# First modulation round of the first layer's mixing: weighted sums on VectorE instead of matmuls on TensorE, at the beginning of the mixing

## The chip, the cores and the metric

The kernel runs on one core of a Trainium2 chip. A core has TensorE (PE in the rows; PEld is its weight load), VectorE (DVE), ScalarE (ACT), GpSimd (POOL) and SyncE (SP), each with an instruction queue of its own that it works through in order; engines wait for one another through semaphores. The metric is the device time of one execution in microseconds.

## What is computed

A diffusion backbone of two layers over 512 latent tokens and 256 context tokens of width 1024, in fp32. Each layer gets six modulation vectors per stream from a small product:

```python
def modulation(cvec, w_mod, b_mod):
    m = (jax.nn.silu(cvec) @ w_mod + b_mod)[..., None, :]
    return jnp.split(m, 6, axis=-1)
...
    sh1, sc1, ga1, sh2, sc2, ga2 = modulation(c, w_mod, b_mod)
    sh1c, sc1c, ga1c, sh2c, sc2c, ga2c = modulation(c_ctx[None], w_mod, b_mod)
    u = (rmsnorm(x, g_mix) * (1 + sc1) + sh1) @ w_in
    ...
    x = x + ga1 * mix
    x = x + ga2 * squared_relu_mlp(rmsnorm(x, g_mlp) * (1 + sc2) + sh2, w_up, w_down)
```

`c` is the conditioning vector of the latent tokens, `c_ctx` that of the context. `w_mod` is 1024x6144 per layer, 24 MB, read for just two vectors. In the middle of a layer stands the mixing: pooling, a bidirectional gated linear attention (GLA) and softmax attention, side by side, on slices of `u`.

## The kernel before, in words

**Tiling.** Activations lie with channels on the partitions (`hT`, eight tiles), each split in a high part, rounded to fp32r, and a low rest; weights are split likewise (`whi` by ScalarE at L159, `wlo` by VectorE at L78), and a product is three matmul passes: high by high, low by high, high by low. `fm_matmul` (L321, L323) gives channel-major results (`fm`, a latent and a context matmul per pass), `tm_matmul` (L340) token-major ones (`tm`).

**Modulation.** It goes in three rounds of two vectors each (2048 columns of `w_mod`). Round 0 (shift and scale of the mixing) of the first layer is computed at the very start. Rounds 1 (mixing gate, MLP shift) and 2 (MLP scale, MLP gate) of the first layer are the thread `mods`, which `mod_rest` makes of two `modulation_round`s (L181): per 128 rows of `w_mod` two tiles `rawm` of 128x1024 are loaded and used at once as the moving operand of four matmuls with the stationary `sstat` (L190), which holds the two conditioning vectors in two of 32 columns; four column groups of the array sum into one PSUM tile `pm`. `mod_end` (L194) adds the bias (`brow`), transposes and writes `modT` and, for a gate, rows in DRAM (`gaD`). The second layer's rounds already go the other way: `modulation_sums` (L211) multiplies and adds the tiles on VectorE into `macc`, one accumulator per stream (the first product by ScalarE, L227, the others L229), and leaves to TensorE just a matmul with a column of ones (`osel`, L238) that sums over the partitions.

**Mixing.** Four threads are written as generators: `"a"` projects (q and k of GLA head pair 1, two gates, then keys and values, queries, pooling), `"g"` is the GLA of both head pairs, `"m"` the modulation, `"t"` the softmax attention. The string `STEPS[0]` names the thread that takes the next step. The steps of `"g"` begin with `decay` (L663) of pair 0, one step per direction: a matmul pair `z` (L670, L671), ScalarE and VectorE in turn (`z`, `e`: L674 to L679), and a tree of products on GpSimd; `levels` (L728) then multiplies the queries by both decays into `QQ` (L771, L772) and computes eight levels of products `att` (L769); the zero level reads `gq` and `KK`, the first one both halves of `QQ`. The gates (`gate_proj`, L642) have a chain of their own on the same engines (`sg`, `gate`).

**What sets the order.** The string gives the order of writing. From it a scheduler with a timeline of its own makes the order of each engine's queue, so work of several threads is interleaved more finely than the string says. Buffers bind it: `wp` holds five tiles each of the tags `hi` and `lo`, shared by weights and `rawm` tiles, and three of `raw`, shared by weights as they come in and `brow`; the accumulators and activations come from 29 tiles of `sp`; of the PSUM pools, `psB` has three tiles and `psA` two. All loads named here stand in SyncE's queue.

Of the kernel before, what the change touches and what calls it, by code (L numbers as in the profile page):

```python
# [10 lines left out]
F32 = mybir.dt.float32  # L11
F32R = mybir.dt.float32r
I32 = mybir.dt.int32
AF = mybir.ActivationFunctionType
ALU = mybir.AluOpType
# [6 lines left out]
KT = 8  # L22
# [2 lines left out]
LEVELS = (1, 2, 4, 8, 16, 32, 64)  # L25
C_GV, C_GG, C_R, C_AQ = 768, 1024, 1280, 1312
GT = 5
STEPS = ("agamagamgaamgaagmaagmagamagamagamagagamagamagamagamgaamgaagmaagmagamagamttgtgttg"
         "tgttgtttgttgttttgttttgtt",
         "aaggggagaggaaagaaggaaaaaagaaaagaaaggaagaaggatatgatttttgaatgt"  # L30
         "tgtttgggtttgttggttttgtttgt")

# [2 lines left out]
def hybrid_kernel(ctx, tc, x, c, cx, c_ctx, w_mod, b_mod, g_mix, w_in, w_pool, s_pool, w_gate, b_gate,  # L35
                  g_gla, g_q, g_k, w_out, g_mlp, w_up, w_down, g_final, k_mask, k_rope, k_edge, k_invw, out):
    nc = tc.nc
    V, A, G, T = nc.vector, nc.scalar, nc.gpsimd, nc.tensor
# [3 lines left out]
    wp = ctx.enter_context(tc.tile_pool(name="wp", bufs=5))  # L42
# [9 lines left out]
    def nm(s):  # L52
        uid[0] += 1
        return f"{s}_{uid[0]}"

    def slot(s, dt=F32, w=NT):
        return sp.tile([128, w], dt, tag="S", name=nm(s))
# [16 lines left out]
    def psC(s):  # L74
        return pc.tile([128, 512], F32, tag="pc", name=nm(s))
# [11 lines left out]
    ident = const.tile([128, 128], F32, name="ident")  # L87
    make_identity(nc, ident)

    osel = const.tile([128, 2, 32], F32, name="osel")  # L90
# [21 lines left out]
    sstat = const.tile([128, KT, 32], F32, name="sstat")  # L112
# [65 lines left out]
    gaD = dp.tile([2, 2, 2, D], F32, name="gaD")  # L178
    xD = dp.tile([NL, D], F32, name="xD")

    def modulation_round(l, r, modT):  # L181
        pm = psC("pm")
        for k in range(KT):
            yield
            for h in range(2):
                raw = wp.tile([128, 1024], F32, tag="lo" if h else "hi", name=nm("rawm"))
                c0 = r * 2048 + h * 1024
                nc.sync.dma_start(raw, w_mod[l, k * 128:(k + 1) * 128, c0:c0 + 1024])
                for j in (2 * h, 2 * h + 1):
                    T.matmul(pm[32 * j:32 * j + 32, :], sstat[:, k, :], raw[:, (j % 2) * 512:(j % 2) * 512 + 512],  # L190
                             start=(k == 0), stop=(k == KT - 1), skip_group_check=True)
        mod_end(l, r, modT, pm)

    def mod_end(l, r, modT, pm):  # L194
        brow = wp.tile([128, 1024], F32, tag="raw", name=nm("brow"), bufs=3)[:, 0:512]
        for j in range(4):
            c0 = r * 2048 + j * 512
            nc.sync.dma_start(brow[32 * j:32 * j + 32], b_mod[l, c0:c0 + 512].partition_broadcast(32))
        V.tensor_tensor(brow, pm, brow, ALU.add)
        pt = psC("pt")  # L200
        for cc in range(4):
            T.transpose(pt[:, cc * 128:(cc + 1) * 128], brow[:, cc * 128:(cc + 1) * 128], ident)
        V.tensor_copy(modT[:, r], pt.rearrange("p (c j r) -> p j c r", c=4, j=4)[:, :, :, 0:2])
        if r >= 1:
            which = r - 1
            for s in range(2):
                for jj in range(2):
                    row = 32 * (jj + (2 if r == 2 else 0)) + s
                    nc.gpsimd.dma_start(gaD[l, which, s:s + 1, jj * 512:(jj + 1) * 512], brow[row:row + 1, :])

    def modulation_sums(l, r, modT, streams):  # L211
# [27 lines left out]
                             start=(s == 0), stop=(s == streams - 1), skip_group_check=True)  # L239
        mod_end(l, r, modT, pm)  # L240

    def mod_vec(modT, idx, s):

        r, j0 = idx // 2, (idx % 2) * 2
        return modT[:, r, j0:j0 + 2, :, s]
# [142 lines left out]
    def fin_scale(l, M, which):  # L388
        modT, scT, shT = M
        o = l * NV + 8 * which  # L390
        g_ = vec[:, o:o + 8].rearrange("p (j c) -> p j c", j=2)
        for s in range(2):
            V.scalar_tensor_tensor(scT[:, which, s].rearrange("p (j c) -> p j c", j=2), mod_vec(modT, 3 * which + 1, s),
                                   1.0, g_, ALU.add, ALU.mult)
            V.tensor_copy(shT[:, which, s].rearrange("p (j c) -> p j c", j=2), mod_vec(modT, 3 * which, s))
# [12 lines left out]
                next(other, None)  # L408

    def mod_rest(l, M):  # L410
        yield from modulation_round(l, 1, M[0])
        yield from modulation_round(l, 2, M[0])
        fin_scale(l, M, 1)

# [9 lines left out]
    for l in range(2):  # L424
# [7 lines left out]
        modT, scT, shT = MODS[l]  # L432
        hT = hT1 if l else new_hT("hT")
        if l == 0:
# [4 lines left out]
            rawm = {}  # L439
# [136 lines left out]


        mods = mod_rest(0, MODS[0]) if both else iter(())
        tstack = ExitStack()
        LT = layer_tables(l, tstack.enter_context(tc.tile_pool(name=f"ta{l}", bufs=1)))  # L580
# [554 lines left out]
        ths = {"g": gla_thread(), "a": at_, "m": mods, "t": att_}  # L1135
        for ch in STEPS[l]:
            if ch == "t":
# [13 lines left out]
        for p2 in range(len(live) // 2):  # L1151
            XP[p2] = bp.tile([128, 2, D], F32, tag=f"X{p2}", name=nm("X"))
            t0 = 2 * p2 * 128
            src = xD[t0:t0 + 256] if l else (x[0, t0:t0 + 256] if p2 < 2 else cx[0])
# [187 lines left out]
```

## Time and profile before

| | us |
|---|---|
| median of 3 runs | 1671.8 |
| lowest, highest | 1671.43, 1680.17 |
| the profiled execution | 1671.28 |
| its span in the profile | 1669.1 |
| mean granted TensorE clock (1 is full) | 0.985 |

The profile is of one execution; times in its rows count from the start of its span. A row of the timeline has the start, the duration, the engine, the line of the kernel, the operation, result and operand by tile names, shapes and count, and in brackets the idle time before it with what ended it. A record is one instruction of the trace; an fp32 matmul leaves two. In the span the first layer's beginning lies from 0 to about 60 us, its mixing from there to about 340, of which the softmax attention starts at about 220.

### The profile page before, as it was taken

To read this page: it belongs to the slowest core of one execution; us is meant where nothing else is said; L and a number is where in the kernel's file an instruction comes from. 1 tells how busy PE (TensorE), PEld (TensorE's weight loads), DVE (VectorE), ACT (ScalarE), POOL (GpSimd) and SP (SyncE) were. 2 spreads that over 40 slices of the span, in tenths; PEclk is the share of its full clock that TensorE was granted. 3 is DMA by queue.
4 is the path that set the end of the run, shared out by engine and by line. 5 is a ranking of instruction groups with operands and counts; after the bars stand their busy time and mean duration, and the time that the engine had idled before them with its cause. 6 is when DMAs were issued, how large, how long until landed. Compare 5 with 4: busy or idle time off the path is not lost.

```text
span 1669.1 us, 27434 instructions
## 1 busy us (share of the span) xinstructions
PE 1595.7 (96%) x11403; PEld 1306.2 (78%) x11403; DVE 923.3 (55%) x1330; ACT 630.9 (38%) x1074; POOL 406.4 (24%) x476
## 2 busy tenths in 40 slices
PE   7999979999999999999999999897999999999997
PEld 4888856678888888888888789785667888888886
DVE  5437666753673654636546563587763545455554
ACT  5545445561531312213113234555662523223332
POOL 1121311212303041130321462241201122222224
PEclk9999989999999999999999999998999999999999
DMA  9445400222340422515424332100032313333331
GB/s 330 128 135 175 149 2 7 98 93 59 102 139 26 141 97 59 176 50 172 150 65 170 103 108 81 40 2 2 33 121 75 111 54 101 101 101 101 101 101 51
DMA packets 136636, 163.31 MB, mean 98 GB/s; under 512 B 9908, under 2 KB 108608, under 8 KB 136512
## 3 DMA queue, kind: packets, MB, share of 16 engines
q1 hardware_dynamic: 130176, 148.41, 27.9%
q10 hardware_dynamic: 5824, 13.12, 2.1%
q8 instruction: 89, 1.46, 0.4%
q14 instruction: 35, 0.29, 0.1%
q0 software_dynamic: 512, 0.03, 0.0%
HBM read 157.31 MB, written 4.23 MB: 97 GB/s over the span
## 4 chain that ended last, share of the span: by engine, by line
PE 84%; DVE 6%; ACT 4%; DMA 2%; issue 2%; POOL 2%; SPq 0%; ACTq 0%; DVEq 0%; POOLq 0%
PE dn L340 25%; PE up L321 19%; PE tm L340 7%; PE op L340 6%; PE up L323 5%; PE fm L321 4%; PE av L1071 3%; PE pT L1054 2%; PE up L330 2%; PE fm L323 1%; PE sc L1033 1%; PE att L769 1%; PE sc L1034 1%; DVE nmx L1036 1%; PE pm L190 1%
## 5 line engine op out<-in xcount | busy, mean ns | idle before, releaser
L159 ACT ACTIVATE whi<-raw 128x1024 fp32r<-128x1024 f32 (+2 forms) x182 | 185.3, 1033 | 568.0 <-PE dn L340 293.0
L1194 POOL TENSOR_TENSOR X<-X,rtmp 128x512 f32<-128x512 f32 x158 | 216.1, 1370 | 640.4 <-DVE rtmp L1193 640.1
L78 DVE TENSOR_TENSOR wlo<-raw,whi 128x1024 fp32r<-128x1024 f32 (+2 forms) x182 | 223.6, 1237 | 213.4 <-ACT whi L159 211.7
L1193 DVE TENSOR_TENSOR rtmp<-dn,ga 128x512 f32<-128x512 f32 x160 | 109.5, 689 | 212.8 <-PE dn L340 211.3
L340 PE MATMUL dn<-whi,ah 128*128 128x512 f32 x480 | 187.3, 390 | 0.6 <-ACT whi L159 0.6
L340 PE MATMUL dn<-whi,al 128*128 128x512 f32 x480 | 187.2, 390 | 0.0
L340 PE MATMUL dn<-wlo,ah 128*128 128x512 f32 x480 | 186.2, 390 | 0.0
L321 PE MATMUL up<-h2h,whi 128*128 128x512 f32 x464 | 182.5, 393 | 1.5 <-ACT relu L1240 1.5
L321 PE MATMUL up<-h2h,wlo 128*128 128x512 f32 x464 | 182.9, 394 | 0.0
L321 PE MATMUL up<-h2l,whi 128*128 128x512 f32 x464 | 182.4, 393 | 0.0
L340 PEld LDWEIGHTS dn<-whi,ah 128*128 128x128 f32 x480 | 90.1, 188 | 22.0 <-ACT whi L159 1.0
L321 PEld LDWEIGHTS up<-h2h,whi 128*128 128x128 f32 x464 | 87.1, 188 | 24.1 <-ACT relu L1240 1.7
L340 PEld LDWEIGHTS dn<-wlo,ah 128*128 128x128 f32 x480 | 90.1, 188 | 19.5 <-DVE wlo L78 0.5
L340 PEld LDWEIGHTS dn<-whi,al 128*128 128x128 f32 x480 | 90.1, 188 | 19.4
L340 PE MATMUL tm<-whi,hTh 128*128 128x256 f32 (+1 forms) x352 | 102.3, 292 | 1.1 <-ACT UV L891 1.1
L321 PEld LDWEIGHTS up<-h2h,wlo 128*128 128x128 f32 x464 | 87.1, 188 | 19.6
L321 PEld LDWEIGHTS up<-h2l,whi 128*128 128x128 f32 x464 | 87.1, 188 | 19.3
L340 PE MATMUL tm<-whi,hTl 128*128 128x256 f32 (+1 forms) x352 | 100.7, 287 | 0.0
L340 PE MATMUL dn<-whi,a 128*128 128x512 f32 x320 | 100.0, 395 | 0.4 <-DVE rtmp L1193 0.4
L340 PE MATMUL tm<-wlo,hTh 128*128 128x256 f32 (+1 forms) x352 | 100.2, 288 | 0.0
L229 DVE SCALAR_TENSOR_TENSOR macc<-rawm,sstat,macc 128x1024 f32<-128x1024 f32 x56 | 76.3, 1383 | 8.2 <-DMA rawm<-in_w_mod_dram 7.7
L1036 DVE TENSOR_REDUCE nmx<-sc 128x1 f32<-128x768 f32 x64 | 60.5, 955 | 24.1 <-PE sc L1034 23.3
(293 smaller groups left out, 3320.6 us busy)
## 6 DMA issues: line engine op xcount, KB each, us to landing
rawm<-in_w_mod_dram SPq DMA_DIRECT2D x80, 512.0 KB, 5.2
raw<-in_w_up_dram SPq DMA_DIRECT2D x64, 512.0 KB, 4.5
raw<-in_w_down_dram SPq DMA_DIRECT2D x64, 512.0 KB, 4.6
raw<-in_w_in_dram SPq DMA_DIRECT2D x26, 512.0 KB, 3.9
rawm<-in_w_mod_dram SPq DMA_DIRECT2D x32, 256.0 KB, 5.3
raw<-in_w_out_dram SPq DMA_DIRECT2D x16, 512.0 KB, 4.7
raw<-in_w_in_dram SPq DMA_DIRECT2D x12, 256.0 KB, 2.8
ga<-gaD ACTq DMA_DIRECT2D x6, 512.0 KB
```

The costliest lines, as they stand in the source:

```text
L78: V.tensor_tensor(lo, full, hi.bitcast(F32), ALU.subtract)
L159: A.activation(hi, raw, AF.Copy)
L229: V.scalar_tensor_tensor(acc[s], raw, c_, acc[s], ALU.mult, ALU.add)
L321: T.matmul(ps[:, 0:NL], a, b[:, 0:NL], start=st, stop=sp_)
L323: T.matmul(ps[:, NL:NT], a, b[:, NL:NT], start=st, stop=sp_)
L330: T.matmul(ps[:, cs], a, b[:, cs], start=(k == 0 and i == 0), stop=(k == nk - 1 and i == 2))
L340: T.matmul(ps, a[:, sl], bb, start=(k == 0 and i == 0), stop=(k == nk - 1 and i == 2))
L1036: V.tensor_reduce(nmx[:, i:i + 1], sv, AX.X, ALU.max, negate=True)
L1054: T.transpose(pt_[:, i * 128:(i + 1) * 128], p_[:, ki * 128:(ki + 1) * 128], ident)
L1071: T.matmul(av_[64 * hh:64 * hh + 64, 0:256], vst, pe[:, hh * 256:hh * 256 + 256], start=(ki == 1), stop=(ki == len(kts) - 2))
L1193: V.tensor_tensor(tmp, ps, ga[0 if t < 4 else 1][:, sl], ALU.mult)
L1194: (V if b == NB - 1 and not both and t == 3 else G).tensor_tensor(X[t][:, sl], X[t][:, sl], tmp, ALU.add)
```

## The change

Round 1 of the first layer is done by a new function, `modulation_half`, twice (mixing gate, then MLP shift, 1024 columns each), in the way of the second layer: per 128 rows of `w_mod` one tile, four weighted sums of 128x512 (two streams, two accumulators each), the first tile's by ScalarE, the seven others' by VectorE; then eight matmuls of 256 columns with the ones-column, bias, two transposes. That is 56 sums on VectorE and 8 first products on ScalarE, and 16 matmuls with ones for the 32 matmuls of round 1. `STEPS[0]` has the steps of `"m"` for this at its front; round 2 stays as it was, on TensorE, with fewer steps and later. Both strings' other parts are the same or moved.

```diff
-STEPS = ("agamagamgaamgaagmaagmagamagamagamagagamagamagamagamgaamgaagmaagmagamagamttgtgttg"
-         "tgttgtttgttgttttgttttgtt",
+STEPS = ("mmmmammgmmammammgmmammgmmaagaagaagagaagaagaagagamagamagamagamgaamgaagmaagmagamag"
+         "amttgtgttgtgttgtttgttgttttgttttgtt",
...
+    def modulation_half(l, r, h, modT):
+
+        acc = [[slot("macc", w=512) for _ in range(2)] for _ in range(2)]
+        c0 = r * 2048 + h * 1024
+        for k in range(KT):
+            raw = wp.tile([128, 1024], F32, tag="lo" if k % 2 else "hi", name=nm("rawm"))
+            nc.sync.dma_start(raw, w_mod[l, k * 128:(k + 1) * 128, c0:c0 + 1024])
+            for s in range(2):
+                c_ = sstat[:, k, s:s + 1]
+                for u in range(2):
+                    src = raw[:, u * 512:u * 512 + 512]
+                    if k == 0:
+                        A.activation(acc[s][u], src, AF.Copy, scale=c_)
+                    else:
+                        V.scalar_tensor_tensor(acc[s][u], src, c_, acc[s][u], ALU.mult, ALU.add)
+            yield
+        brow = wp.tile([128, 1024], F32, tag="raw", name=nm("brow"), bufs=3)[:, 0:256]
+        pm = psC("pm")
+        for j in range(4):
+            nc.sync.dma_start(brow[32 * j:32 * j + 32], b_mod[l, c0 + j * 256:c0 + j * 256 + 256].partition_broadcast(32))
+            for s in range(2):
+                T.matmul(pm[32 * j:32 * j + 32, 0:256], osel[:, s], acc[s][j // 2][:, (j % 2) * 256:(j % 2) * 256 + 256],
+                         start=(s == 0), stop=(s == 1), skip_group_check=True)
+        V.tensor_tensor(brow, pm[:, 0:256], brow, ALU.add)
+        pt = psC("pt")
+        for cc in range(2):
+            T.transpose(pt[:, cc * 128:(cc + 1) * 128], brow[:, cc * 128:(cc + 1) * 128], ident)
...
-        yield from modulation_round(l, 1, M[0])
+        yield from modulation_half(l, 1, 0, M[0])
+        yield from modulation_half(l, 1, 1, M[0])
```

What this does to the queues is seen in three places. First VectorE, before the change, around the two decays of head pair 0 (`e`, `z`), the gates' chain (`sg`, `gate`) and the scaled queries `QQ`:

```order
L771 TENSOR_TENSOR QQ_1163<-gq_771,z_1057 128x768
L675 SCALAR_TENSOR_TENSOR e_1148<-z_1147 128x768
L652 TENSOR_SCALAR sg_1134<-gate_1133 128x768
L678 SCALAR_TENSOR_TENSOR z_1147<-z_1147,e_1148 128x768
L656 SCALAR_TENSOR_TENSOR gate_1133<-sg_1134,vec,gate_1133 128x768
L772 TENSOR_TENSOR QQ_1163<-gq_771,z_1147 128x768
L726 TENSOR_TENSOR KK_773<-KK_773,z_1147 128x384
L78 TENSOR_TENSOR wlo_1623<-raw_1620,whi_1622 128x1024
L78 TENSOR_TENSOR wlo_1629<-raw_1626,whi_1628 128x1024
```

and the same place in the changed kernel (`macc` are the new sums, `brow` the second half's result):

```order
L256 SCALAR_TENSOR_TENSOR macc_1077<-rawm_1283,sstat,macc_1077 128x512
L256 SCALAR_TENSOR_TENSOR macc_1078<-rawm_1283,sstat,macc_1078 128x512
L78 TENSOR_TENSOR wlo_1734<-raw_1731,whi_1733 128x1024
L808 TENSOR_TENSOR QQ_1280<-gq_771,z_1158 128x768
L78 TENSOR_TENSOR wlo_1740<-raw_1737,whi_1739 128x1024
L712 SCALAR_TENSOR_TENSOR e_1265<-z_1264 128x768
L689 TENSOR_SCALAR sg_1247<-gate_1246 128x768
L265 TENSOR_TENSOR brow_1289<-pm_1290,brow_1289 128x256
L271 COPY modT_124<-pt_1304 128x8 x2
L431 COPY shT_126<-modT_124 128x8 x2
L715 SCALAR_TENSOR_TENSOR z_1264<-z_1264,e_1265 128x768
L693 SCALAR_TENSOR_TENSOR gate_1246<-sg_1247,vec,gate_1246 128x768
```

The 56 sums and two more lowerings of weights (the first queries') now stand ahead of the second decay's `e`, and the second half's result in the middle of that decay.

Second TensorE at the first level of products (`att` with `QQ`), before:

```order
L340 MATMUL tm_1326<-whi_1179,hTh_141 128x256
L340 MATMUL tm_1326<-whi_1179,hTl_142 128x256
L340 MATMUL tm_1326<-wlo_1180,hTh_141 128x256
L769 MATMUL att_1353<-QQ_1163,KK_773 32x32 x48
L340 MATMUL tm_1416<-whi_1173,hTh_127 128x256
```

and in the changed kernel (`pm_1290` is the second half's sum by the ones-column, `pm_2111` round 2):

```order
L263 MATMUL pm_1290<-macc_1076,osel 32x256
L263 MATMUL pm_1290<-macc_1078,osel 32x256
L806 MATMUL att_1382<-gq_771,KK_773 32x32 x22
L268 MATMUL pt_1304<-ident,brow_1289 128x128 x2
L190 MATMUL pm_2111<-rawm_2178,sstat 32x512 x2
L190 MATMUL pm_2111<-rawm_2182,sstat 32x512 x2
L806 MATMUL att_1488<-QQ_1280,KK_773 32x32 x9
L376 MATMUL tm_1461<-whi_1316,hTh_127 128x256
```

Before, the first level stood behind the fourth token tile of keys and values; now it stands behind the third, right after the zero level (`att` with `gq`), the second half's end and four matmuls of round 2.

Third SyncE's loads, before, from the second q and k weights (`raw_881`, `raw_938`) on; `raw_996` and `raw_1078` are the gates', `raw_1171` the first of keys and values:

```order
L152 DMA raw_881<-in_w_in_dram 128x8x128
L152 DMA raw_938<-in_w_in_dram 128x8x128
L152 DMA raw_996<-in_w_in_dram 128x8x128
L152 DMA raw_1078<-in_w_in_dram 128x8x128
L188 DMA rawm_1136<-in_w_mod_dram 128x1024
L152 DMA raw_1171<-in_w_in_dram 128x4x256
```

and in the changed kernel the piece with the gates' (`raw_1085`, `raw_1191`), behind `raw_909`, `raw_990` and the first `rawm` tiles:

```order
L248 DMA rawm_977<-in_w_mod_dram 128x1024
L248 DMA rawm_983<-in_w_mod_dram 128x1024
L248 DMA rawm_1079<-in_w_mod_dram 128x1024
L152 DMA raw_1085<-in_w_in_dram 128x8x128
L152 DMA raw_1191<-in_w_in_dram 128x8x128
L248 DMA rawm_1149<-in_w_mod_dram 128x1024
L248 DMA rawm_1143<-in_w_mod_dram 128x1024
L248 DMA rawm_1174<-in_w_mod_dram 128x1024
```

Nine `rawm` tiles now precede the gates' weights, and sixteen those of keys and values.

More of the change, by code (lines that the diff above doesn't have):

```diff
@@ L240, in modulation_sums @@
         mod_end(l, r, modT, pm)
+    def modulation_half(l, r, h, modT):
[24 more added lines that the diff above has]
+            T.transpose(pt[:, cc * 128:(cc + 1) * 128], brow[:, cc * 128:(cc + 1) * 128], ident)
+        src = pt[:, 0:256].rearrange("p (c j r) -> p j c r", c=2, j=4)
+        for a in range(2):
+            V.tensor_copy(modT[:, r, 2 * h + a].rearrange("p (b c) s -> p b c s", b=2), src[:, 2 * a:2 * a + 2, :, 0:2])
+        if (r, h) in ((1, 0), (2, 1)):
+            for s in range(2):
+                for j in range(4):
+                    nc.gpsimd.dma_start(gaD[l, r - 1, s:s + 1, j * 256:(j + 1) * 256], brow[32 * j + s:32 * j + s + 1, :])
+        yield
     def mod_vec(modT, idx, s):
```

## The prediction

> **What bounds the kernel now.** Read first: the page's busy line and the shares by engine of the chain of waits.
>
> ```profile
> PE 1595.7 (96%) x11403; PEld 1306.2 (78%) x11403; DVE 923.3 (55%) x1330; ACT 630.9 (38%) x1074; POOL 406.4 (24%) x476
> PE 84%; DVE 6%; ACT 4%; DMA 2%; issue 2%; POOL 2%; SPq 0%; ACTq 0%; DVEq 0%; POOLq 0%
> ```
>
> TensorE carries 84% of the chain, so matmuls taken away should shorten it, but only where TensorE is what is waited for. Second, the busy times by stretch: start:end, length, then busy us (instructions) of PE, PEld, DVE, ACT and POOL, the granted clock, DMA share, GB/s.
>
> ```profile
> 60.00:130.00 70.00, 70.00 (x645) 59.76 (x644) 24.34 (x29) 29.61 (x46) 10.15 (x16) 1.00 0.49 154
> 130.00:160.00 30.00, 28.71 (x665) 24.45 (x664) 21.90 (x47) 14.84 (x36) 5.29 (x8) 1.00 0.39 127
> 160.00:220.00 60.00, 59.83 (x784) 47.47 (x784) 36.94 (x78) 26.31 (x45) 19.48 (x32) 1.00 0.41 137
> 220.00:240.00 20.00, 13.68 (x380) 10.15 (x366) 17.68 (x33) 9.62 (x18) 5.53 (x13) 0.74 0.02 4
> 240.00:260.00 20.00, 16.19 (x241) 11.90 (x241) 12.10 (x23) 13.12 (x35) 0.00 (x0) 0.83 0.01 2
> ```
>
> From 60 to 220, the mixing's first part, TensorE is never free (158.5 of 160 us) and VectorE has 45.7 free of the first 70. So the move goes from the bound engine to one with room. The question is whether VectorE still answers in time while it does the work: its queue is strictly in order.
>
> **What TensorE is rid of.** Round 1 of the modulation is 32 matmuls (64 records; each fp32 matmul leaves two). The timeline of PE around one block of 8 records and around the one of 24:
>
> ```profile
> 80.85 0.28 PE L323 MATMUL fm<-hTh,wlo 128*128 128x256 f32 x1
> 81.06 1.06 PE L190 MATMUL pm<-rawm,sstat 128*32 128x512 f32 x8
> 82.05 0.50 PE L321 MATMUL fm<-hTh,whi 128*128 128x512 f32 x1
> 82.39 0.28 PE L323 MATMUL fm<-hTh,whi 128*128 128x256 f32 x1
> ...
> 118.96 0.28 PE L340 MATMUL tm<-wlo,hTh 128*128 128x256 f32 x1
> 119.17 3.74 PE L190 MATMUL pm<-rawm,sstat 128*32 128x512 f32 x24
> ...
> 123.06 0.28 PE L340 MATMUL tm<-whi,hTl 128*128 128x256 f32 x1
> ```
>
> Starts lie 0.12 us apart for 256 columns and 0.235 for 512. From 80.85 to 82.39 are 1.54 us; without the block they would be 0.12+0.235, so it costs 1.19 with its hiccups. The long one costs 4.10-2x0.12=3.86. Round 1 is five short blocks and the long one: 5x1.19+3.86=**9.8 us** (8.6 at least, if the hiccups stay).
>
> **What TensorE gets.** Two times eight ones-matmuls of 256 columns. The nearest row is the second layer's, four matmuls (8 records) of 512 columns, two column groups side by side:
>
> ```profile
> 552.51 0.28 PE L323 MATMUL up<-h2h,wlo 128*128 128x256 f32 x1
> 552.73 1.91 PE L238 MATMUL pm<-macc,osel 128*32 128x512 f32 x8
> ...
> 554.90 0.28 PE L323 MATMUL up<-h2h,whi 128*128 128x256 f32 x1
> ```
>
> 2.39-0.355=2.0 us for four of 512, so as much for eight of 256. The new order sends both streams' matmuls of one column group behind each other, so again about two run side by side. Two halves and one hiccup (the first half is split in two): **4.2 us**; 2.0 if four groups overlapped as in round 1's own blocks, 8.1 if none did. Transposes: two pairs instead of four in one go, nothing. TensorE's work falls by 9.8-4.2=**5.6 us**.
>
> **What VectorE gets.** 56 products-and-sums of 128x512, none of which stands in the trace. Neighbours: the second layer's, twice as wide, by timeline; then, by groups of the first 420 us (count, busy us, mean ns), the plain lowerings, a product of 128x512, and a product-and-difference of 64x512.
>
> ```profile
> 464.14 2.48 DVE L229 SCALAR_TENSOR_TENSOR macc<-rawm,sstat,macc 128x1024 f32<-128x1024 f32 x2
> 466.54 0.95 DVE L78 TENSOR_TENSOR al<-relu,ah 128x768 fp32r<-128x768 f32 x1
> ...
> L78 DVE TENSOR_TENSOR wlo<-raw,whi 128x1024 fp32r<-128x1024 f32 x23 | 28.2, 1233 | 25.5 <-ACT whi L159 25.2
> L1162 DVE TENSOR_TENSOR rtmp<-op,ga 128x512 f32<-128x512 f32 x9 | 6.1, 690 | 24.3 <-PE op L340 24.3
> L970 DVE SCALAR_TENSOR_TENSOR pm<-pl,invw,pl 64x512 f32<-64x512 f32 x4 | 3.0, 748 | 0.4 <-POOL pl L969 0.3
> ```
>
> A pair of wide ones takes 2.40 to the next start, 1.20 each; 512 columns fewer are worth 1.233-0.690=0.54: **0.67 us** each (0.60, half the wide one, to 0.80, above the 0.748 as it stands). 56 make 37.5 us, against the 45.7 free. As a total it fits. As an order it does not, and that is the crux.
>
> **VectorE's queue up to the second decay.** The scheduler put the sums between the lowerings of weights, all of them before the second gate decay of head pair 0. That decay is on TensorE's path: its operations e, sg, z, gate (VectorE and ScalarE in turn) end in the scaled query QQ, and the first level of GLA products on TensorE reads both halves of QQ. In the trace of before, by timeline:
>
> ```profile
> 59.16 0.28 PE L323 MATMUL fm<-hTh,wlo 128*128 128x256 f32 x1
> 72.28 0.50 PE L321 MATMUL fm<-hTh,whi 128*128 128x512 f32 x1
> 110.95 0.40 PE L670 MATMUL z<-rT,wg 96*128 96x512 f32 x1
> 125.90 1.06 PE L769 MATMUL att<-QQ,KK 64*32 64x32 f32 x96
> ...
> 101.83 0.56 DVE L652 TENSOR_SCALAR sg<-gate 128x768 f32<-128x768 f32 x1
> 107.03 1.58 DVE L771 TENSOR_TENSOR QQ<-gq,z 128x768 f32<-128x768 f32 x1
> 112.79 0.96 DVE L675 SCALAR_TENSOR_TENSOR e<-z 128x768 f32<-128x768 f32 x1 [4.17 <-ACT z L674]
> 119.09 1.58 DVE L772 TENSOR_TENSOR QQ<-gq,z 128x768 f32<-128x768 f32 x1
> ...
> 116.92 0.47 ACT L785 ACTIVATE dg<-att 128x384 f32<-128x384 f32 x1
> ...
> DMA to landing us min/median/max: 3.5/5.3/6.4
> ```
>
> The second e starts at 112.79, QQ ends at 120.67, TensorE reads it at 125.90: 5.2 us to spare. Now the same e in the changed order. The first w_mod tiles can be issued when TensorE frees the first q and k weights' buffers at 59.4; the second, the first that VectorE sums, lands 3.5 to 6.4 later, say 65.0. From there stand before e:
>
> - 56 sums x 0.67 = 37.5
> - eight lowerings at 1.233 less 0.09 of overlap = 9.1
> - the first decay, e, sg, z, gate and QQ, near 0.9+0.5+0.9+0.9+1.5 = 4.7
> - the low part of rT, one sum of the round's result, small copies: 1.4, estimated from the 0.69 of a 512-wide operation
>
> 52.7 us. Two waits: the third tile takes the first one's buffer, so it is issued only after ScalarE has read that one four times and lands near 69.5 (1.7 us idle); and the first half's result waits for its ones-matmuls (0.5). So e starts near 119.9, 7 us late. From e to the end of QQ were 7.9 us with the dg copy of 0.47 between; dg now stands on ScalarE ahead of it, 7.4. QQ is ready near **127.3**.
>
> When does TensorE want it? The second z comes at 110.95 - 1.2 (the block at 81) - 19x0.12 (19 of 25 token-major matmuls now behind z) + 2.0 (first ones-matmuls) + 0.3 (their transposes) + 0.3 (a wait, below) = 110.1. Then z 0.35, 66 matmuls 7.9, the second ones-matmuls 2.0, the zero-level products 1.0: 121.4. The second half's transposes wait for VectorE, which has brow behind e and sg: 121.9, **0.5** lost. Four round-2 matmuls, 1.2: at 123.5 TensorE stands before the first-level products, and waits until 127.3: **3.8 us** (0 to 8, as VectorE's queue is 4 us shorter or longer). Behind them in its queue stand the token-major matmuls, so nothing fills the gap; these could not start either, since ScalarE empties their PSUM only after the same decay.
>
> Smaller edits. The second q weights' lowering stands behind the third tile's sums, ready near 73.3 where TensorE wants it at 73.0: **0.3** (0 to 2). On SyncE nine w_mod tiles now precede the gate weights and sixteen the k weights; by the same landing times and buffer releases they are in place near 85, 95 and 102 where TensorE wants them at 90, 101 and 100 (high part by 99), so the queue hides it with 1 to 5 us. GpSimd sends eight small rows instead of four, long before they are read: nothing.
>
> **The clock.** A gap on TensorE costs more than itself:
>
> ```profile
> 241.12 0.49 PE L1054 MATMUL pT<-ident,p 128*128 128x128 f32 x3
> ...
> 245.44 0.90 PE L1054 MATMUL pT<-ident,p 128*128 128x128 f32 x3 [2.66 <-ACT p L1037]
> ```
>
> The same three transposes take 0.49 before and 0.90 after an idle time of 2.66; and the granted clock of 0.83 from 240 to 260 is 6.8 us at half (0.17x2x20), that of 0.74 before it 10.4 us. A gap of 3.8 should do the same; some 5 us of dense matmuls at half pace lose **2.5 us** (0 if the gate does not fall, 5.2 for the longer spell). The Trainium skill (TensorE: Matmul & The Clock Gate, "What's actually happening") says that the array falls to half clock after an idle window of about 3.4 us and needs a busy one to come back; by that a gap under 3.4 could pass free and the sum would be 2.5 less. The trace, with 2.66, has it fall earlier.
>
> **The sum.** -9.8+4.2+0.3+0.5+3.8+2.5=**+1.5 us**. After the wait the rest of the stage has the same matmuls, and TensorE is again the bound until 220. The profiled execution took 1671.28 (span 1669.1), 0.5 under the median 1671.8, so I forecast 1671.8+1.5=**1673.3**: no change. About 0.5%, 8.4 us, is what a measurement of this kernel can tell from none, so the lines lie at 1663.4 and 1680.2.
>
> **Rivals.**
>
> *The cover holds.* If a sum takes 0.60, VectorE's queue is 3.9 us shorter, QQ is ready at 123.4 and TensorE does not stop. For: half of 1.20 is 0.60; 45.7 us were free. Against: the 0.748 of the narrower one. Then -9.8+4.2+0.3+0.2=-5.1: 1666.7. Chance 0.20.
>
> *The backlog grows.* Every us that VectorE is later is one more before the first-level products, with no filler; then the k weights' second lowering, 1.3 us ahead of its matmul, comes late too. It decides "slower" from 6.9 us more: 56 sums of 0.79, or four more tiles that arrive like the third. For: the landing times reach 6.4 and each matrix has five buffers; L771 takes 1.58 where a 768-wide operation takes 0.96, and GpSimd was at work beside it. Against: the 512-wide rows. With 8 us: 1681. Chance 0.17. The Trainium skill (SBUF — State Buffer, "SBUF: two separate sides") says that a VectorE instruction with two SBUF inputs and a GpSimd one that reads SBUF shut each other out for a whole instruction; each sum is of that kind, so by the page some of GpSimd's 10.15 us of this stretch would come on top.
>
> *The wait comes, the clock holds.* The gap passes without half clock: 1673.3-2.5=1670.8. For: from 60 to 220 the pauses (1.5 us in all) left the clock at 1.00. Against: none of those pauses was near 3.8, and 2.66 was enough at 245. Chance 0.13.
>
> **How the numbers follow.** Forecast 0.50. Low end: the first rival, 1666.7, with 0.7 for cheaper ones-matmuls: 1666. High end: into the second, 1682, as the softmax stage's order also changes a little (a half-clock spell more or less there is 2 to 3 us). Faster needs more than the first rival has, 0.04; slower is most of the second, 0.15; same 0.81.
>
> **What would show it.** Right: L190 down to 64 records; the new sums near 0.75 long and 0.67 apart; VectorE without idle time from 70 to 119; e of the second decay near 120 instead of 112.8; TensorE idle for 3 to 5 us ahead of the first-level products, released by QQ; then matmuls at double length. Wrong: TensorE without a gap before 130 (first rival); gaps ahead of gate or k matmuls, released by the lowering (second); or a difference that only arises after 220.

## The result and the profile after

| | us |
|---|---|
| changed kernel, median of 5 runs | 1686.09 (1683.88 to 1689.8) |
| kernel before, median of 5 runs | 1672.67 (1671.43 to 1680.17) |
| ratio, 95% interval | 1.0077 [1.0066, 1.0089] |
| profiled execution after, its span | 1687.76, 1685.7 |

The change costs 13.4 us, where 1.5 were forecast. The page of the changed kernel, busy line and shares of the chain:

```profile
PE 1600.7 (95%) x11371; PEld 1310.7 (78%) x11371; DVE 961.5 (57%) x1390; ACT 636.4 (38%) x1082; POOL 415.7 (25%) x480
PE 83%; DVE 6%; ACT 4%; DMA 4%; issue 2%; POOL 2%; SPq 0%; ACTq 0%; DVEq 0%; POOLq 0%
```

DMA's share of the chain has gone from 2% to 4%: some transfers are now waited for. TensorE's busy time is 5 us higher although it has 32 records less; at a lower clock the same work stays busy longer (the `kbt` rows below, six records each, take 0.88 and, behind a gap, 1.39). By stretches:

```profile
60.00:130.00 70.00, 64.94 (x512) 54.87 (x510) 59.21 (x85) 34.98 (x48) 17.48 (x20) 0.99 0.66 208
130.00:160.00 30.00, 28.25 (x651) 27.19 (x652) 21.42 (x44) 10.78 (x27) 6.17 (x11) 0.92 0.22 64
160.00:220.00 60.00, 55.95 (x760) 43.25 (x760) 37.52 (x78) 29.36 (x59) 17.73 (x28) 0.97 0.32 107
```

TensorE, before free for 1.5 us of these 160, is now free for 10.9, and the granted clock, 1.00 before, is 0.99, 0.92 and 0.97. VectorE went from 24.34 to 59.21 in the first stretch. That more is loaded there (208 GB/s instead of 154) costs nothing by itself: in e9 below, with the same loads and no sums, it is 215 GB/s, and TensorE is busy for all of these 70 us.

Where does the difference arise? Two marks bound the stage that the change touches: the second transposes of the parameters (`pv`), ahead of which no matmul has changed, and the first transposed key (`kT`). In the timeline of before, then of the changed kernel:

```profile
72.11 0.24 PE L140 MATMUL pv<-ident,prow 23*128 23x23 f32 x1
...
221.30 0.87 PE L990 MATMUL kT<-ident,UK 128*128 128x128 f32 x6
```

```profile
73.81 0.24 PE L140 MATMUL pv<-ident,prow 23*128 23x23 f32 x1
...
233.62 0.87 PE L1027 MATMUL kT<-ident,UK 128*128 128x128 f32 x6
```

From mark to mark are 149.2 us before and 159.8 after. **This stage is the measure in what follows**, since start and rest also vary between executions of one kernel (below). What TensorE waits for in it, by the waits of the changed kernel from 72 to 240 (total, times, longest):

```profile
PE att L806 <- DVE QQ L809: 5.0, 1, 5.0
PE pm L190 <- DMA rawm<-in_w_mod_dram: 2.9, 2, 2.4
```

Neither wait is in the kernel before. The first is the wait that was predicted, ahead of the first level of products. Its place on TensorE:

```profile
124.84 1.06 PE L190 MATMUL pm<-rawm,sstat 128*32 128x512 f32 x8 [0.38 <-PE pt L268]
130.91 0.42 PE L806 MATMUL att<-QQ,KK 64*32 64x32 f32 x18 [5.01 <-DVE QQ L809]
131.26 0.58 PE L376 MATMUL tm<-whi,hTh 128*128 128x256 f32 x1
131.64 0.41 PE L376 MATMUL tm<-whi,hTl 128*128 128x256 f32 x1
131.85 0.41 PE L376 MATMUL tm<-wlo,hTh 128*128 128x256 f32 x1
...
134.62 0.36 PE L376 MATMUL tm<-whi,hTh 128*128 128x256 f32 x1
134.83 0.28 PE L376 MATMUL tm<-whi,hTl 128*128 128x256 f32 x1
134.94 0.28 PE L376 MATMUL tm<-wlo,hTh 128*128 128x256 f32 x1
```

Up to 134.62 the matmuls behind the gap start 0.21 apart instead of 0.12: half clock. VectorE and ScalarE in the same time:

```profile
87.25 8.04 DVE L256 SCALAR_TENSOR_TENSOR macc<-rawm,sstat,macc 128x512 f32<-128x512 f32 x12
...
122.22 0.94 DVE L712 SCALAR_TENSOR_TENSOR e<-z 128x768 f32<-128x768 f32 x1
...
129.27 1.58 DVE L809 TENSOR_TENSOR QQ<-gq,z 128x768 f32<-128x768 f32 x1
```

```profile
117.84 0.90 ACT L711 ACTIVATE z<-z,vec 128x768 f32<-128x768 f32 x1
123.83 0.49 ACT L822 ACTIVATE dg<-att 128x384 f32<-128x384 f32 x1 [5.09 <-PE att L806]
124.21 0.83 ACT L713 ACTIVATE e<-e 128x768 f32<-128x768 f32 x1
```

ScalarE has `z` ready at 118.7, VectorE gets to `e` only at 122.22, behind the sums and lowerings, each sum 0.67 from the next. Then ScalarE, held up by `dg`, takes `e` at 124.21, and the last `QQ` ends at 130.85.

The second wait was not predicted. Round 2 on TensorE, two of its rows from the kernel before, then the changed kernel with the transposed keys (`kbt`) that follow:

```profile
164.78 1.92 PE L190 MATMUL pm<-rawm,sstat 128*32 128x512 f32 x16
...
171.36 1.06 PE L190 MATMUL pm<-rawm,sstat 128*32 128x512 f32 x8
```

```profile
166.68 1.06 PE L190 MATMUL pm<-rawm,sstat 128*32 128x512 f32 x8
...
169.31 1.05 PE L190 MATMUL pm<-rawm,sstat 128*32 128x512 f32 x4 [0.49 <-DMA rawm<-in_w_mod_dram]
172.80 1.92 PE L190 MATMUL pm<-rawm,sstat 128*32 128x512 f32 x4 [2.44 <-DMA rawm<-in_w_mod_dram]
174.65 1.39 PE L737 MATMUL kbt<-ident,KK 128*128 128x128 f32 x6
175.97 1.05 PE L190 MATMUL pm<-rawm,sstat 128*32 128x512 f32 x4
176.96 0.88 PE L737 MATMUL kbt<-ident,KK 128*128 128x128 f32 x6
```

The tiles come late because SyncE waits for their buffers, which the key and value weights hold until the token-major matmuls are done (its queue's waits from 110 to 200):

```profile
SPq L188 <- PE tm L376: 30.5, 3, 19.9
```

And the rows show something else: a block of 4 records, that is one tile, takes as long as one of 8. From start to next start, waits left out, round 2's 64 records take 7.8 us in 7 blocks before and 11.9 in 11 blocks in the changed kernel, 0.9 of it by half clock.

### The profile page after: what moved, and what is told of

Same layout as the page of the kernel before. It is cut to its first block, busy times and chain, and to the rows that moved or that the text cites. A ratio compares the mean times of both kernels' runs of the same rounds, so it can differ in the third digit from the quotient of the medians.

```text
span 1685.7 us, 27463 instructions
## 1 busy us (share of the span) xinstructions
PE 1600.7 (95%) x11371; PEld 1310.7 (78%) x11371; DVE 961.5 (57%) x1390; ACT 636.4 (38%) x1082; POOL 415.7 (25%) x480
## 4 chain that ended last, share of the span: by engine, by line
PE 83%; DVE 6%; ACT 4%; DMA 4%; issue 2%; POOL 2%; SPq 0%; ACTq 0%; DVEq 0%; POOLq 0%
PE dn L376 24%; PE up L357 19%; PE tm L376 7%; PE op L376 6%; PE up L359 5%; PE fm L357 3%; PE av L1108 3%; PE pT L1091 2%; PE up L366 2%; DMA rawm<-in_w_mod_dram 2%; PE sc L1070 1%; PE fm L359 1%; PE att L806 1%; PE sc L1071 1%; DVE nmx L1073 1%
```

## The experiments

All times of the table are read from timelines: the stage from `pv` to `kT`, and TensorE's idle time in it (pauses of 0.15 us and more between one matmul's end and the next one's start). Each profile is of one execution. "Ratio" is to the kernel before on the same chip, with its 95% interval; its median there was 1673.75 for e1 to e4, 1675.25 for e5 and e6, 1674.01 for e9 to e11 and 1674.05 for e12 to e14.

| kernel | median us | ratio | stage | idle |
|---|---|---|---|---|
| before; a second profile | 1672.67 | | 149.2; 148.3 | 1.3; 0.5 |
| changed; a second profile | 1686.09 | 1.0077 [1.0066, 1.0089] | 159.8; 159.2 | 10.8; 9.8 |
| e1 string only | 1680.28 | 1.0038 [1.0024, 1.0052] | 152.9 | 2.6 |
| e2 28 sums | 1674.58 | 1.0003 [0.9993, 1.0014] | 148.4 | 4.8 |
| e3 round 2 in other buffers | 1710.06 | 1.0217 [1.0199, 1.0234] | 184.3 | 15.1 |
| e4 second half late | 1683.84 | 1.0061 [1.0039, 1.0083] | 159.3 | 12.3 |
| e5 sums, old string | 1682.48 | 1.0048 [1.0035, 1.0062] | 158.6 | 11.6 |
| e6 one half | 1678.12 | 1.0019 [1.0009, 1.0029] | 149.2 | 3.0 |
| e9 no sums | 1674.06 | 0.9996 [0.9984, 1.0008] | 149.5 | 4.0 |
| e10 42 sums | 1673.96 | 0.9994 [0.9980, 1.0009] | 150.8 | 4.2 |
| e11 second half very late | 1691.06 | 1.0096 [1.0076, 1.0116] | 150.7 | 6.0 |
| e12 no sums, old string | 1667.41 | 0.9962 [0.9947, 0.9976] | 145.1 | 2.8 |
| e13 round 2 in four groups | 1679.96 | 1.0033 [1.0021, 1.0045] | 155.2 | 7.6 |
| e14 one half, four groups | 1674.4 | 1.0008 [0.9995, 1.0021] | 153.6 | 5.6 |

**e1, the string alone.** Round 1 stays on TensorE, over as many steps as the changed kernel gives it.

```diff
-        yield from modulation_half(l, 1, 0, M[0])
-        yield from modulation_half(l, 1, 1, M[0])
+        for n, _ in enumerate(modulation_round(l, 1, M[0])):
+            yield
+            if n:
+                yield
+        for _ in range(3):
+            yield
```

> Round 1 back as 32 matmuls on TensorE, with the changed order of steps kept (its steps spread over the same 18 places); no sums on VectorE. Theory A (two waits, each with half clock behind it: the first-level products wait 5.0 us for the second decay, which the sums made late; the round-2 tiles wait for buffers, 2.9 us, which the order of steps made late): the first wait is gone, the second stays, TensorE has its 9.8 us again: about 1677 us, second e before 115, a wait of 2 to 3 us for a w_mod tile ahead of the state transposes. Rival B (the order of steps does all of it, the sums are free): 5 us above the changed kernel, about 1690. Rival C (the late decay does all of it): as before, 1672, and no wait for w_mod tiles.

6.5 us slower, without a sum on VectorE, and 4.2 of it in the stage: with round 1 on TensorE, the order of steps costs two fifths of what the whole change costs there. The wait for `QQ` is gone, the one for round-2 tiles stays:

```profile
PE pm L190 <- DMA rawm<-in_w_mod_dram: 1.9, 2, 1.6
```

Round 2 takes 11.0 us in 11 blocks, without half clock (the stage's granted clock is 1.00): 3.1 more than before; with the wait, that covers the 4.2.

**e2, half of the sums.** The second stream keeps only its first product.

```diff
-                    else:
+                    elif s == 0:
                         V.scalar_tensor_tensor(acc[s][u], src, c_, acc[s][u], ALU.mult, ALU.add)
```

> Leaves out the context stream's sums but for the first product: 28 sums instead of 56, VectorE's queue shorter by 28 x 0.665 = 18.6 us, everything else as in the changed kernel. A: second e before 115, no wait ahead of the first-level products, no half clock there, the wait for round-2 tiles stays: 1686 less 8, about 1678. B: 1686. C: 1672 or less, 1667 if the 5.6 us of spared TensorE work show.

As fast as before, with the changed order of steps: 28 sums fewer are worth 11.1 us of the stage. The waits for round-2 tiles stay (1.7), and theory A had 1678 for that; TensorE's lighter work (143.6 us of the stage without idle time, instead of 147.9) makes up for its idle time.

**e3, other buffers for round 2**, so that no weight holds up its tiles: 128x512 pieces from the accumulators' 29 tiles.

```diff
-                raw = wp.tile([128, 1024], F32, tag="lo" if h else "hi", name=nm("rawm"))
...
+                    raw = slot("rawm", w=512)
+                    o = c0 + (j % 2) * 512
+                    nc.sync.dma_start(raw, w_mod[l, k * 128:(k + 1) * 128, o:o + 512])
```

> The changed kernel with round 2's tiles in the activations' pool, as four tiles of 128x512 per 128 rows, so that they no longer wait for weights to free the hi and lo buffers. A: the wait for the decay stays (4 to 5 us), that for w_mod tiles goes, with its half clock: 1686 less 4 to 5, about 1681. B: the round-2 tiles are the whole: about 1673. C: 1686.

A miss, and the most telling one. Round 2 was torn into single matmuls, two records each, as the pieces came in. The timeline of this kernel's TensorE:

```profile
199.24 1.05 PE L191 MATMUL pm<-rawm,sstat 128*32 128x512 f32 x2
200.22 0.38 PE L377 MATMUL tm<-whi,hTl 128*128 128x256 f32 x1
```

A single matmul holds TensorE for 0.98 us, as long as four that run side by side in the four column groups. Its 64 records stood in 27 blocks and took 28.0 us; before, round 2's 64 took 7.8. So late buffers were not tested alone: the cure was worse than they are.

**e4, the second half after the levels' begin.**

```diff
-STEPS = ("mmmmammgmmammammgmmammgmmaagaagaagagaagaagaagagamagamagamagamgaamgaagmaagmagamag"
-         "amttgtgttgtgttgtttgttgttttgttttgtt",
+STEPS = ("mmmmammgmmamagagaagmaagmaagmagmaagmaagmaagmagmmamagamagamagamgaamgaagmaagmagamagamttgtgttgtgttgtttgttgttttgttttgtt",
```

> The same sums, but the second half's steps (MLP shift) written between the later projections instead of in front, so that fewer sums stand ahead of the second decay's e; round 2 correspondingly a little later. A: second e near 114, first-level products not waiting for it, round-2 tiles still late in part: 1668 to 1676. B: about 1684, as the sums' place is of no matter. C: 1667 to 1672.

The wait for `QQ` of the second decay is gone, and the first level starts 5.0 us earlier within the stage than in the changed kernel. All of it is lost again, in many smaller waits (`kbt` for `KK` 2.9, a transpose for a late tile 2.7, `att` for `KK` 1.9, ones-matmuls for `macc` 1.8), most of them for VectorE, which is now full where the levels need its answers. Its stretch from 130 to 160:

```profile
130.00:160.00 30.00, 26.67 (x567) 24.46 (x565) 30.00 (x58) 11.50 (x23) 0.00 (x0) 1.00 0.60 207
```

**e5, the sums under the old string**, two tiles to a step.

```diff
+        for h in range(2):
+            for n, _ in enumerate(modulation_half(l, 1, h, M[0])):
+                if n % 2:
+                    yield
```

> The other half of the change: the sums on VectorE, two tiles to a step, under the old string of steps, so that the second half's sums spread over the products' levels and round 2 keeps nearly its old place. Theory A (the loss is made where sums stand in front of the second decay and round 2 arrives late; TensorE itself is 4.4 us lighter): no QQ wait near 125, no wait for round-2 tiles near 170, between 1666 and 1673. Theory B (the sums on VectorE cost by themselves, wherever they stand): about as slow as the changed kernel, 1680 to 1688. Theory C (the string costs 6 us by itself, the sums 6 by themselves and the two add up): 1679 to 1681.

Theory A fell: no `QQ` wait, no wait for a round-2 tile over 0.2, and the stage is 158.6 all the same, with waits of 2.4 (`kbt` for `KK`), 2.3, 2.0, 1.8 and 1.4. VectorE's 130 to 160 is full here too:

```profile
PE kbt L739 <- DVE KK L765: 2.4, 1, 2.4
130.00:160.00 30.00, 28.02 (x521) 25.43 (x522) 30.00 (x59) 11.58 (x23) 1.91 (x4) 0.95 0.63 213
```

So it is not one unlucky place. Round 2 takes 12.0 us here as well, though the old string has it in its old place: four of its eight blocks are single tiles, and half clock falls on others.

**e6, one half** on VectorE; the other on TensorE, each tile as four matmuls of 256 columns.

```diff
+        for n, _ in enumerate(modulation_half(l, 1, 0, M[0])):
...
+        for n, _ in enumerate(modulation_half(l, 1, 1, M[0], True)):
...
+                T.matmul(pm[32 * j:32 * j + 32, 0:256], sstat[:, k, :], raw[:, j * 256:j * 256 + 256],
```

> As the run before, but only the mixing gate's half of round 1 on VectorE (28 sums); the MLP shift's half stays on TensorE as matmuls of 256 columns. Theory A (VectorE's backlog decides): no wait for QQ, TensorE only some 2 us lighter than in the kernel before, so 1668 to 1675. Theory B: half of the changed kernel's loss, 1677 to 1681. Theory C: sums alone cost 0.1 us each, so 1675 to 1677.

The stage is as long as before: with half of the matmuls gone and 28 sums, idle time is 3.0 instead of 0.5 to 1.3, as much as the work is shorter (146.1 us without idle time instead of 147.9). The median, in theory B's range, is 2.9 us above the kernel before; by the profile that lies outside the stage.

**e7 and e8, both kernels once more**, for a second profile.

> The kernel before, unchanged, for a second profile. In the first, the last vector of round 0 came 1.4 to 2.3 us earlier than in all changed kernels, before any changed work, and its second layer had 1 to 4 us less of half clock though its waits were the same. If these are differences of the execution, this profile shows a start or a second layer that lies between; if they belong to the kernel, it repeats the first within 0.3 us.

> The changed kernel, unchanged, for a second profile. What belongs to the kernel comes again: the 5.0 us wait for QQ, 2.4 us for a round-2 tile near 172, half clock behind both. The start (1.7 us late) and the second layer (4.3 us more) come again within 0.5 us if they belong to the kernel, and differ by more if they belong to the execution.

The second `pv` came at 72.11 and 74.76 in the kernel before, at 73.81 and 75.71 in the changed one, and everywhere between in the others: the start belongs to the execution. The stages repeat within 0.9 us. Behind `kT` follow 1447.8 and 1449.9 us before, 1452.0 and 1452.6 after; but also 1452.8 (e6), 1452.1 (e1), 1449.1 (e5), 1446.7 (e12). That does not go with the sums or with the string.

**e9 and e10, without sums, and with 42 of 56** (for e10 the second stream gets sums in one accumulator only).

```diff
-                    else:
+                    elif k < 1:
```

> The changed kernel without its 56 sums on VectorE: only the 8 first products by ScalarE remain, with all loads and the ones-matmuls; the round's result is wrong by the sums left out. From the second start of the parameter transposes (near 74) to the first transposed key the kernel before took 148 to 149 us, the changed one 159 to 160. Theory A (waits for VectorE cost all that was lost, TensorE is 4 to 5 us lighter): 144 to 146 in this stage, 1667 to 1671 in all. Theory B (loads and buffers of the tiles, with round 2's later place, cost most of it): 150 or more, 1675 and above.

> The changed kernel with 42 of its 56 sums (one of the second stream's two accumulators gets only its first product; the result is wrong by that). With 28 the stage took 148.4 us, with 56 159.8. Theory A (a queue that is full from some point on: below it sums are free, above it each costs its 0.67 us and more): 149 to 154, 1674 to 1680 in all. Theory B (each sum costs alike, 0.4 us): 154, 1680. Theory C (the cost comes with a step, as a gap long enough for half clock): either within 1 us of 28 sums or within 2 of 56.

The stage over the number of sums, under the new string: 149.5 (none), 148.4 (28), 150.8 (42), 159.8 (56). So there is, in this order of steps, a point from which the queue is full. With 42, `e` still starts 1.2 us after ScalarE has `z` ready (at 115.4), but `QQ` ends at 124.58, 1.6 us before TensorE reads it:

```profile
116.56 1.10 DVE L712 SCALAR_TENSOR_TENSOR e<-z 128x768 f32<-128x768 f32 x1
...
123.00 1.58 DVE L809 TENSOR_TENSOR QQ<-gq,z 128x768 f32<-128x768 f32 x1
```

14 sums more are 9.4 us of queue, and `e` comes 5.7 later (4.5 counted from `pv`). But e9, between its two theories and nearer to B, leaves a riddle: no sum at all, TensorE lighter, and no gain.

**e11, the second half in the softmax attention**, behind round 2.

```diff
+        yield from modulation_round(l, 2, M[0])
+        for n, _ in enumerate(modulation_half(l, 1, 1, M[0])):
```

> A version that could beat both: the old string's order, the mixing gate's half summed on VectorE early (28 sums, two tiles a step), then round 2 on TensorE, and the MLP shift's 28 sums in the softmax attention behind it, where TensorE waits for others anyway. Theory A (VectorE has room for 28 sums in the early stage and 28 in the late one): the stage to the first transposed key at 145 to 147 us, and 1669 to 1672 in all. Theory B (the softmax stage also waits for VectorE's and ScalarE's answers, and the sums stand in their way): the stage as in A, the part behind it 4 to 10 us longer, 1675 to 1681.

Theory B, and worse. The stage is 150.7 where both theories had 145 to 147, with a wait of 3.1 for ScalarE: here 28 sums may not have been free (no run has this string without them). And behind `kT` the kernel loses 13 us up to the first output matmul. There TensorE waits for the softmax's `pe` 6.7 us in three waits, in the kernel before 2.3 in one. In this kernel and then in before, waits from 222 to 400:

```profile
PE av L1112 <- DVE pe L1107: 6.7, 3, 3.8
```

```profile
PE av L1071 <- DVE pe L1066: 2.3, 1, 2.3
```

**e12, no sums under the old string**, the answer to the riddle (e5's kernel with e9's edit).

> The changed kernel's loads and ones-matmuls without the 56 sums, under the old string of steps, where round 2 stands in blocks of 8 and 16 records (the result is wrong by the sums left out). With the new string and no sums the stage from the second parameter transposes to the first transposed key took 149.5 us, in the kernel before 148 to 149. Theory A (the relief was given back by round 2, late and in blocks of 4 records that cost as much as 8): the stage at 141 to 145, 1665 to 1669 in all. Theory B (the relief is lost whatever round 2 does, since TensorE then waits for the answers of ScalarE and VectorE in the levels): 147 to 150, 1671 to 1675.

Theory A, with the stage a hair outside its range: the relief is there, 6.6 us in all and 3.7 in the stage, if round 2 stays in blocks of 8 and 16 records and in time. Where the other 2.9 arise was not traced. Compare the two timelines. Without sums under the new string (e9):

```profile
159.91 1.05 PE L190 MATMUL pm<-rawm,sstat 128*32 128x512 f32 x4 [1.00 <-DMA rawm<-in_w_mod_dram]
161.84 1.53 PE L190 MATMUL pm<-rawm,sstat 128*32 128x512 f32 x4 [0.89 <-DMA rawm<-in_w_mod_dram]
163.30 1.54 PE L737 MATMUL kbt<-ident,KK 128*128 128x128 f32 x6
```

and under the old one (e12):

```profile
165.94 1.06 PE L190 MATMUL pm<-rawm,sstat 128*32 128x512 f32 x8
```

Round 2 takes 11.9 us of TensorE in 11 blocks there (0.9 of it by half clock, behind two gaps of 1.0 and 0.9) and 9.3 in 7 here, the ones-matmuls 3.0 in three blocks there and 2.1 in two here.

**e13, round 2 in four column groups** in the changed kernel, all sums kept.

```diff
-        yield from modulation_round(l, 2, M[0])
+        for h in range(2):
+            for n, _ in enumerate(modulation_half(l, 2, h, M[0], True)):
+                if n % 2:
+                    yield
```

> The changed kernel with all its sums; only round 2 differs: two halves of 1024 columns, each tile as four matmuls of 256 columns, one to a column group. Theory A (blocks of one tile that fill two of four column groups cost some 3 us, the late tiles' waits 3 more): round 2's matmuls at 7 to 8 us instead of 11.9, the wait for QQ as before, the stage at 154 to 157, 1680 to 1683 in all. Theory B (round 2 plays no part): 159 to 160, 1684 to 1688.

Theory A: 5.9 us above the kernel before instead of 13.4. A lone tile now takes 0.64 instead of 1.05 by its row, and no longer fills the time by itself:

```profile
167.66 0.64 PE L251 MATMUL pm<-rawm,sstat 128*32 128x256 f32 x8 [1.22 <-DMA rawm<-in_w_mod_dram]
169.37 0.64 PE L251 MATMUL pm<-rawm,sstat 128*32 128x256 f32 x8 [1.07 <-DMA rawm<-in_w_mod_dram]
```

Round 2 takes 9.2 us (7 to 8 were expected), the tiles are waited for as long as before (2.9), and the wait of the second decay (3.8) has moved to a token-major matmul ahead of the products, which waits for ScalarE to empty a PSUM tile behind the same decay. Since the order of the queues changed too, the 4 us of the stage can't be split cleanly.

**e14, one half, all tiles in four groups**, meant to beat both.

> 28 sums (mixing gate) on VectorE under the old string, everything else of rounds 1 and 2 on TensorE with four matmuls of 256 columns to a tile: a version that could beat both. Theory A: TensorE some 3 us lighter than before, waits of 2 to 3 us as with one half alone: the stage at 146 to 148, 1670 to 1674. Theory B (waits in the levels set the pace): 149 to 150, 1674 to 1678.

Same as before by the median, at the border of the two theories (1674); the interval of its ratio holds 1. The profile says little: its execution took 1680.93, 6.5 above the median, TensorE stands 3.6 us ahead of products for no cause that the trace names, and the stage, 153.6, is outside both theories. No kernel that computes everything beat the kernel before.

## Why the prediction was wrong

The stage gives three terms, each between two kernels whose source differs in just that (for before and the changed kernel the mean of two profiles, 148.8 and 159.5). The scheduler makes all queues anew for each kernel, so no term is quite alone:

| | predicted us | measured us | between |
|---|---|---|---|
| round 1's matmuls off TensorE | -5.6 | -3.7 | before, e12 |
| the new order of steps | 0 | +4.4 | e12, e9 |
| the 56 sums | +7.1 | +10.0 | e9, changed |
| sum | +1.5 | +10.7 | |

The sizes of the last two terms hang on which comes first. Taken the other way, from e12 to e5 the sums cost 13.5 under the old string, and from e5 to the changed kernel the new order adds only 0.9. Both tear round 2 apart and make TensorE wait, so what is shown is their sum, 14.4, and that each alone can do most of the harm.

**TensorE's relief: right as a sum.** Stage less idle time is 147.9 before and 142.3 in e12: 5.6 us of work gone, as worked out; 1.9 come back as idle time (the longest waits are 1.2 for ScalarE and 0.7 for VectorE's `KK`). The exact agreement is partly luck: in e12 the ones-matmuls cost 2.1, in whole blocks, not 4.2, and round 2 1.5 more. In the changed kernel the ones-matmuls cost 4.1, as forecast, but for another reason: torn into five blocks.

**The sums' queue: right in kind and place, short in size.** A sum takes 0.67 (forecast 0.67). `e` came at 122.22 in a profile that started 1.7 late, so 120.5 against 119.9; TensorE stood ready at 125.9, so 124.2 against 123.5 (the terms named for it make 123.1). From `e` to the end of `QQ` I gave 7.4, arguing that `dg` now stood on ScalarE ahead of it; it took 8.6. `dg` does stand ahead, but it waits for the products until 123.83 and holds `e` back; the gate's chain takes turns on top. The wait is 5.0 (4.9 in the second profile) instead of 3.8. The half clock behind it cost 1.65 (from 131.26 to 134.83 stand 16 starts, 3.57 us instead of 16 x 0.12), less than the 2.5 for one gap, but there were two gaps: behind the 2.44 the 4 records take 1.92 instead of 1.05 and `kbt` 1.39 instead of 0.88, 1.4 more. The Trainium skill's rule that I weighed (TensorE: Matmul & The Clock Gate, "What's actually happening": half clock after an idle window of about 3.4 us) fits neither gap: the 2.44 us gap is shorter and was followed by half clock all the same, and in the 5.01 the clock fell after about 2 us (last section).

**The step that failed** is the sentence after the sum: "After the wait the rest of the stage has the same matmuls, and TensorE is again the bound until 220." The number of matmuls was the same, but round 2 had moved behind round 1's tiles and the weights in SyncE's queue and the buffers. I followed SyncE only for the weights that come sooner, not for the tiles that come later. Its matmuls came one tile at a time, two column groups at a time, for the price of four: 11.9 us instead of 7.8. And TensorE waited 2.9 us for tiles (2.6 in the second profile). The forecast put both at nothing. The stage came out 9.2 us longer than forecast: in the changed kernel itself TensorE's idle time grew by 9.4 where 4.6 were forecast, and its work by 1.3 where 3.1 less was forecast. The 4.1 of round 2 are most of the second difference; the tiles' 2.6 to 2.9 and 1.2 of the longer wait for `QQ` are most of the first. With the new order of steps, and no sums on VectorE, the stage is 4.2 longer (before to e1) and 4.4 (e12 to e9), more than the 3.7 that the relief brings; in e13, with all sums but lone tiles made cheaper, it is 4.3 shorter. My rows had blocks of 8 and 24 records; I had none with four and did not ask for one.

**The rivals.** "The cover holds" counted on 3.9 us less of queue; with 9.4 less, at 42 sums, the wait is gone, but not the rest: that stage is still 2.0 longer than before, where the rival had 5.1 less. "The backlog grows" had the right side and too narrow a mechanism: it priced a later `QQ`, which came 1.9 us later than forecast, and missed the order of steps. "The clock holds" did not happen. That VectorE and GpSimd shut each other out (the Trainium skill, SBUF — State Buffer, "SBUF: two separate sides") shows at most here and there: the two sums during the tree of products on GpSimd at 117.30 took 1.74 together, two undisturbed ones 1.41.

**What stays open.** Of the 13.4 us 10.7 lie in the stage; the rest lies behind `kT`, where the changed kernel's two profiles have 3.4 us more than those of before. Kernels of both kinds lie on either side there, so what sets it was not found. Of the sums' 10.0 us between e9 and the changed kernel, 6.3 are idle time (10.3 against 4.0), 1.6 half clock behind the long gap and 1.1 the ones-matmuls' torn blocks; 1 us is not traced. How much each of the two terms would cost with every queue otherwise the same was not measured.

## What to carry to other kernels

Work moved off the bound engine pays only as far as the engine that takes it still answers in time: count how much of its queue stands ahead of each answer, and look for the amount up to which it costs little (here 42 sums of 56, with 1.3 us of the stage over none, in the new order of steps), because beyond it the stage paid in all three places where the 56 sums were put (the changed kernel, e4, e5). A move changes the order of everything that shares its queue, its buffers and its steps; follow what is pushed back as carefully as what is pulled ahead, and price matmuls that fill the array in part by the block, not by the record.

## What was not expected of the hardware

The time of a block of fp32 matmuls with 32-column stationaries is that of one column group: 0.98 to 1.00 us from start to next start for 512 columns, with one group (e3, 2 records), two (4 records) or four (8 records); 0.57 for four groups of 256 columns (e13, e14). So two of four groups left empty cost half of TensorE for that time, and the order in which tiles land decides it.

Half clock sets in while TensorE still waits. By the windows of the changed kernel:

```profile
127.00:135.00 8.00, 4.09 (x36) 4.03 (x37) 5.17 (x5) 3.95 (x10) 4.34 (x7) 0.57 0.20 52
135.00:139.00 4.00, 4.00 (x105) 3.81 (x105) 2.08 (x6) 1.39 (x3) 0.00 (x0) 1.00 0.32 95
```

A clock of 0.57 over 8 us is 6.9 us at half, but TensorE was idle for 3.9 of the 8. The matmuls are at full pace again from 134.83, so the half clock began at about 128, 2 us after the gap's start at 125.9. So the spell cost 1.65 us and not half of 6.9. The gap of 2.44 cost 1.4: half as long, and about as dear. Nor does the length of a gap alone decide: behind one of 1.9 in e6 the granted clock is 0.66 from 121 to 126, behind one of 1.9 in e2 it stays at 1.00 (83 to 90).
